# Splits of the weight chunks queued behind the building of the down activations in a fused encoder block

## The chip, the cores and the metric

The kernel runs on one core of one Trainium2 chip, in one launch. The metric is the device time of that launch in microseconds (us), lower is better. Several runs were timed, and one further execution was taken with the hardware profiler.

## The reference

One residual block over 512 tokens of width 1024, all in float32. `rms_norm` divides a row by its root mean square and multiplies by a gain.

```
f = swiglu(rms_norm(h, g_ffn1_pre), w_ffn1_gate, w_ffn1_up, w_ffn1_down)
h = h + 0.5 * rms_norm(f, g_ffn1_post)
u = rms_norm(h, g_mix_pre);  q_a, k_a, v_a, q_b, k_b, v_b = split(u @ w_in)
o_a = stick_breaking_attention(q_a, k_a, v_a);  o_b = chunk_band_attention(q_b, k_b, v_b, rel_bias)
h = h + rms_norm(concat(rms_norm(o_a), rms_norm(o_b)) @ w_out, g_mix_post)
f = swiglu(rms_norm(h, g_ffn2_pre), w_ffn2_gate, w_ffn2_up, w_ffn2_down)
h = h + 0.5 * rms_norm(f, g_ffn2_post)
h = h + rms_norm((p @ w_ple_proj) * sigmoid(h @ w_ple_gate), g_ple_post)

swiglu(x, wg, wu, wd) = (silu(x @ wg) * (x @ wu)) @ wd      # 1024 -> 2816 -> 1024
```

The change touches the two feed-forward stages, called FFN1 and FFN2 here; both go through the same code.

## The kernel before

**Precision.** Each float32 operand is split into a high part, rounded to the fast matmul format fp32r, and a low part, the rest. `split_to` (L311) makes both: ScalarE (ACT) casts the high part (L313), then VectorE (DVE) subtracts it from the source to get the low part (L314). `mm3` (L247) issues three matmuls on TensorE (PE): high weights by high activations (L248), high by low (L249), low by high (L250). The low part of a weight is therefore first needed by the third matmul of a product.

**Weight chunks.** Weights come in chunks of 128 x 1024 (some 128 x 768). `emit_dma` (L168) loads a chunk from SyncE's queue (SP) into a raw tile `wr`, `wx` or `wy`; `emit_split` (L192) splits it into `wh` and `wl`, of which there are four buffers each. Some chunks are sums of weight blocks: once the raw tile has been split, `sum_in` (L222) issues a DMA from GpSimd's queue (POOL, L223) that adds another block into the same raw tile, and the result is split again as a later chunk. `ensure` (L227) issues loads and splits ahead of use; it is called at the end of each product, for the chunk three products ahead (`LOOK`, L25).

**The products.** The 22 blocks of 128 hidden columns of a feed-forward are worked in four groups (L39): four plain blocks, then nine pairs of blocks. A pair's gate and up projection is a 2 x 2 block product in the seven-product form, operands `U0` to `U6`; each product is 24 matmuls of 128 x 256. The products of one pair, in the order 0, 1, 2, 4, 3, 6, 5 (L44), are interleaved with those of the next pair: after product 5 of pair p come product 4 of pair p+1, product 0 of pair p+2, product 3 of pair p+1, product 1 of pair p+2, product 6 of pair p+1. PE runs its instructions in exactly this order. Products 0, 3, 6 and 5 of a pair accumulate in one PSUM bank (`f_a`), product 1 uses `f_b`, products 2 and 4 use `f_c`.

After certain products the banks are read out: L592 and L593 (gate, first half), L596, L599 (`f_x`: ACT copies `f_c`, DVE adds `f_a`), L605, and after product 5 the SiLU of L609 and the multiplication of L646, which completes `f_b`, the hidden activations of the pair (DVE tile `f_b`, not the PSUM bank). A product that accumulates again into a bank has to wait until its reader is done: product 6 waits for L599, product 5 for L605.

**Building the down activations.** The down projection of the middle two groups, three pairs each, also goes by seven products, run from `down_product` (L626). Its activation operands `V` are built by `keep_blocks` (L486), once for each of the six pairs and twice in the kernel: a split of the halves `b4[:, 0::2]` (L499, two tiles of 128 x 256, possible as soon as L646 has written the first half, some products earlier), four differences `f_vw` on DVE (L501 to L503, one after the other), the split of these four into `f_v` (L504, 128 x 1024) and a split of one block into `f_vsl` or `f_vsh` (L505, 128 x 256). The operands of the first two pairs of a group are used many products later; those of the third pair begin to be used two products after product 5 of that pair, since product 0 of the down projection comes after product 4 of the next pair. If the operands of the group before are still in use, the split work of a pair waits for them (`kept`, L563); that is so for the fourth pair, the first of the second group.

**What sets the order.** Only PE's order is written out by hand. On ACT, DVE and POOL a scheduler picks the order from a model of the timeline at build time, and each engine then runs its instructions in that order. `behind` (L321) adds the rule that the instructions inside it stand, on the same engine, after given ones; it adds no wait between engines. `emit_split` uses it so that a chunk's split stands behind `marks["evac"]`, the read-out of the latest product:

```
        for q in range(cuts):
            a, b = q * n // cuts, (q + 1) * n // cuts
            with behind("evac"):
                marks["split"] = split_to(hi[:, a:b], lo[:, a:b], r[:, a:b])
```

The functions that the change touches, and what calls them:

## Time and profile before

| | us |
|---|---|
| median of three runs | 1000.22 |
| lowest and highest of the three | 997.71 and 1000.41 |
| the profiled execution, its own time | 1002.25 |
| its span, first to last instruction | 1000.5 |

The time holds 1.75 us outside the span of the profiled execution. In that span FFN1's pairs and down products run from about 64 to 260 us and those of FFN2 from about 655 to 860 us; attention lies between. The names in a row are the program's tiles with buffer numbers left out: `wl<-wx,wh` is the low part of a chunk, made from its raw tile and its high part. A row of the timeline gives start, duration, engine, line, operation, output and inputs, and in brackets how long the engine stood idle before it and what it waited for. The next instruction of DVE or ACT often starts some 0.1 us before the end of the one before, if it doesn't need its result.

### The profile page before, as it was taken

How to read it: one execution, taken by the hardware profiler on the slowest of the kernel's cores; microseconds unless marked ns; L12 is line 12 of the kernel's file. 1: busy time of each engine (PE TensorE's matmuls, PEld its weight loads, DVE VectorE, ACT ScalarE, POOL GpSimd, SP SyncE). 2: the span in 40 equal slices, each digit the busy share in tenths (PEclk: the TensorE clock that was granted, in tenths of full speed). 3: DMA queues.
4: the chain of work that ended last, by engine and by line, in shares of the span. 5: the costliest groups of instructions: out<-in, count | busy, mean ns of one | idle time of the engine just before them, and what ended most of it. 6: DMA issues, size and time to landing. Idle time of an engine off the chain costs nothing.

```text
span 1000.5 us, 18453 instructions
## 1 busy us (share of the span) xinstructions
PE 980.4 (98%) x7242; PEld 922.5 (92%) x7242; DVE 775.3 (77%) x1357; ACT 585.8 (59%) x979; POOL 134.5 (13%) x221
## 2 busy tenths in 40 slices
PE   9999999999999999999999999999999999999996
PEld 7889999999999999888898899899999999999885
DVE  6777787677667788999999767796776787676857
ACT  6446654564455467777789655565643664555563
POOL 0001112122210004343000000011122122210000
PEclk9999999999999999999999999999999999999999
DMA  7348888988896132313332402269789888975202
GB/s 280 102 106 189 170 188 183 207 181 177 211 191 206 60 82 88 89 61 102 99 89 92 139 10 65 61 142 204 149 186 204 181 169 212 195 180 185 64 1 85
DMA packets 44855, 139.71 MB, mean 140 GB/s; under 512 B 5216, under 2 KB 5600, under 8 KB 44768
## 3 DMA queue, kind: packets, MB, share of 16 engines
q0 software_dynamic: 14976, 50.34, 30.5%
q1 hardware_dynamic: 28368, 85.83, 25.3%
q10 hardware_dynamic: 1424, 2.36, 0.9%
q8 instruction: 57, 0.93, 0.4%
q14 instruction: 30, 0.25, 0.1%
HBM read 134.31 MB, written 2.10 MB: 136 GB/s over the span
## 4 chain that ended last, share of the span: by engine, by line
PE 75%; DMA 8%; DVE 8%; ACT 4%; issue 4%; POOL 0%; SPq 0%; DVEq 0%; POOLq 0%; ACTq 0%
PE f_a L248 7%; PE f_a L250 7%; PE f_a L249 7%; PE f_c L248 3%; PE f_c L250 3%; PE f_c L249 3%; PE pj L248 3%; PE pj L249 3%; PE pj L250 3%; DMA wy<-in_wst_dram 3%; DVE wl L314 2%; PE pt L937 2%; PE f_d L250 2%; PE f_d L249 2%; PE f_d L248 2%
## 5 line engine op out<-in xcount | busy, mean ns | idle before, releaser
L314 DVE TENSOR_TENSOR wl<-wx,wh 128x1024 fp32r<-128x1024 f32 (+1 forms) x104 | 118.3, 1139 | 39.6 <-ACT wh L313 38.7
L313 ACT CAST wh<-wx 128x1024 fp32r<-128x1024 f32 (+1 forms) x104 | 101.8, 985 | 68.1 <-DMA wx<-in_wst_dram 37.4
L314 DVE TENSOR_TENSOR wl<-wr,wh 128x1024 fp32r<-128x1024 f32 (+2 forms) x100 | 109.3, 1099 | 28.8 <-ACT wh L313 28.1
L313 ACT CAST wh<-wr 128x1024 fp32r<-128x1024 f32 (+2 forms) x100 | 94.3, 950 | 46.0 <-DMA wr<-in_wgu_dram 14.0
L223 POOL DMA_DIRECT2D wx<-in_wst_dram x54 | 47.1, 872 | 403.8 <-DVE wl L314 339.5
L313 ACT CAST wh<-wy 128x1024 fp32r<-128x1024 f32 (+1 forms) x52 | 51.4, 988 | 47.5 <-DMA wy<-in_wdst_dram 23.7
L314 DVE TENSOR_TENSOR wl<-wy,wh 128x1024 fp32r<-128x1024 f32 (+1 forms) x52 | 59.2, 1139 | 15.8 <-ACT wh L313 15.2
L248 PE MATMUL pj<-um_hi,wh 128*128 128x512 f32 (+1 forms) x160 | 56.7, 355 | 1.2 <-DVE f_f L658 1.1
L249 PE MATMUL pj<-um_lo,wh 128*128 128x512 f32 (+1 forms) x160 | 55.7, 348 | 0.1
L250 PE MATMUL pj<-um_hi,wl 128*128 128x512 f32 (+1 forms) x160 | 55.8, 348 | 0.0
L248 PE MATMUL f_a<-f_U6h,wh 128*128 128x256 f32 x144 | 40.0, 278 | 2.0 <-DVE f_x L599 1.3
L248 PE MATMUL f_a<-f_U0h,wh 128*128 128x256 f32 x144 | 40.0, 278 | 0.0
L249 PE MATMUL f_a<-f_U0l,wh 128*128 128x256 f32 x144 | 39.8, 277 | 0.0
L250 PE MATMUL f_a<-f_U0h,wl 128*128 128x256 f32 x144 | 39.8, 277 | 0.0
L248 PE MATMUL f_b<-f_U1h,wh 128*128 128x256 f32 x144 | 39.8, 277 | 0.0
L249 PE MATMUL f_b<-f_U1l,wh 128*128 128x256 f32 x144 | 39.8, 277 | 0.0
L250 PE MATMUL f_b<-f_U1h,wl 128*128 128x256 f32 x144 | 39.8, 277 | 0.0
L248 PE MATMUL f_c<-f_U2h,wh 128*128 128x256 f32 x144 | 39.8, 277 | 0.0
L249 PE MATMUL f_c<-f_U2l,wh 128*128 128x256 f32 x144 | 39.8, 277 | 0.0
L250 PE MATMUL f_c<-f_U2h,wl 128*128 128x256 f32 x144 | 39.8, 277 | 0.0
L248 PE MATMUL f_a<-f_U5h,wh 128*128 128x256 f32 x144 | 39.8, 277 | 0.0
L249 PE MATMUL f_a<-f_U5l,wh 128*128 128x256 f32 x144 | 39.8, 277 | 0.0
(461 smaller groups left out, 3851.3 us busy)
## 6 DMA issues: line engine op xcount, KB each, us to landing
wx<-in_wst_dram POOLq DMA_DIRECT2D x54, 512.0 KB, 5.7
wx<-in_wst_dram SPq DMA_DIRECT2D x18, 512.0 KB, 4.9
wy<-in_wst_dram SPq DMA_DIRECT2D x18, 512.0 KB, 5.8
wr<-in_wst_dram SPq DMA_DIRECT2D x18, 512.0 KB, 5.8
wy<-in_wst_dram POOLq DMA_DIRECT2D x18, 512.0 KB, 5.8
wx<-in_wdst_dram POOLq DMA_DIRECT2D x24, 384.0 KB, 5.5
wr<-in_wqk_dram SPq DMA_DIRECT2D x16, 512.0 KB, 3.7
wr<-in_wgu_dram SPq DMA_DIRECT2D x15, 512.0 KB, 4.2
```

Of the source, the lines that this page charges most:

```text
L223: pool.dma_start(out=r, in_=block, accum_op=ALU.add)
L248: pe.matmul(ps, hi, mh, start=start, stop=False, skip_group_check=skip)
L249: pe.matmul(ps, hi, ml, start=False, stop=False, skip_group_check=skip)
L250: pe.matmul(ps, lo, mh, start=False, stop=stop, skip_group_check=skip)
L313: a = act.copy(hi, src)
L314: b = dve.tensor_tensor(lo, src, hi.bitcast(F32), ALU.subtract)
L937: pe.transpose(pt[:, qi * P:(qi + 1) * P], aw[qi][:, (j - qi) * P:(j - qi + 1) * P], ident[:])
```

## The change

```
@@ emit_split
         for q in range(cuts):
             a, b = q * n // cuts, (q + 1) * n // cuts
-            with behind("evac"):
+            with behind("evac", "kept"):
                 marks["split"] = split_to(hi[:, a:b], lo[:, a:b], r[:, a:b])
@@ keep_blocks
-            split_to(e2[:, 0], e2[:, 1], b4[:, 0::2])
+            parts = split_to(e2[:, 0], e2[:, 1], b4[:, 0::2])
             w = half4(unit(f"vw{g}{r}", "b", 3))
             dve.tensor_tensor(w[:, 0:2], b4[:, 0::3], b4[:, 1:2].broadcast_to([P, 2, HT]), ALU.subtract)
             dve.scalar_tensor_tensor(w[:, 2], w[:, 1], -1.0, b4[:, 0], ALU.mult, ALU.subtract)
             dve.scalar_tensor_tensor(w[:, 3], w[:, 2], -1.0, b4[:, 2], ALU.mult, ALU.subtract)
-            split_to(e4[:, 0], e4[:, 1], w)
-            split_to(e1[:, 0], e1[:, 1], b4[:, 3:4])
+            parts += split_to(e4[:, 0], e4[:, 1], w)
+            marks["kept"] = parts + split_to(e1[:, 0], e1[:, 1], b4[:, 3:4])
```

Every split of a weight chunk that is traced after a call of `keep_blocks` now stands, on ACT and on DVE, behind the three casts and the three low parts of that call. No instruction is added or removed and no size changes. PE, POOL and SP keep their orders; ACT and DVE get new ones around ten of the twelve builds, and in the two builds of a fourth pair only the small split of L505 moves up, ahead of one chunk's split.

On ACT, after the product 5 of the first pair of FFN1 (the SiLU of L609), the rows are these; `wh_1070` is the chunk of the product 3 that comes three products later, `wh_1099` and `wh_1128` those of the two products after it:

```order
 L609 ACTIVATE f_g_1050<-f_a_667 128x512
+L313 CAST f_vsl_1056<-f_b_920 128x256
+L599 COPY f_x_1156<-f_c_994 128x512
+L313 CAST f_v_1053<-f_vw_1060 128x1024
 L313 CAST wh_1070<-wx_762 128x1024
 L313 CAST wh_1099<-wr_1068 128x1024
-L313 CAST f_vsl_1056<-f_b_920 128x256
 L313 CAST wh_1128<-wy_956 128x1024
-L599 COPY f_x_1156<-f_c_994 128x512
 L313 CAST wh_1161<-wx_987 128x1024
-L313 CAST f_v_1053<-f_vw_1060 128x1024
```

The casts of the build, and with them the read-out `f_x` of the next pair's bank `f_c`, have moved ahead of the four chunks.

On DVE at the same place, behind L501 of the build, `wl_1071` is the low part of that first chunk:

```order
+L314 TENSOR_TENSOR f_vsl_1056<-f_b_920,f_vsl_1056 128x256
+L502 SCALAR_TENSOR_TENSOR f_vw_1060<-f_vw_1060,f_b_920 128x256
+L503 SCALAR_TENSOR_TENSOR f_vw_1060<-f_vw_1060,f_b_920 128x256
+L314 TENSOR_TENSOR f_v_1053<-f_vw_1060,f_v_1053 128x1024
 L314 TENSOR_TENSOR wl_1071<-wx_762,wh_1070 128x1024
-L502 SCALAR_TENSOR_TENSOR f_vw_1060<-f_vw_1060,f_b_920 128x256
 L314 TENSOR_TENSOR wl_1100<-wr_1068,wh_1099 128x1024
-L314 TENSOR_TENSOR f_vsl_1056<-f_b_920,f_vsl_1056 128x256
-L503 SCALAR_TENSOR_TENSOR f_vw_1060<-f_vw_1060,f_b_920 128x256
 L314 TENSOR_TENSOR wl_1129<-wy_956,wh_1128 128x1024
-L314 TENSOR_TENSOR f_v_1053<-f_vw_1060,f_v_1053 128x1024
 L599 TENSOR_TENSOR f_x_1156<-f_a_864,f_x_1156 128x512
```

The whole build now stands ahead of the three low parts that it was woven into, and the read-out L599 stays behind all of them.

On DVE in the build of the third pair of FFN1, again behind L501, the down projection's accumulation L637 comes in as well; `wl_1539` is the chunk of the product 3 three products later:

```order
+L314 TENSOR_TENSOR f_vsh_1057<-f_b_1393,f_vsh_1057 128x256
+L502 SCALAR_TENSOR_TENSOR f_vw_1528<-f_vw_1528,f_b_1393 128x256
+L503 SCALAR_TENSOR_TENSOR f_vw_1528<-f_vw_1528,f_b_1393 128x256
+L314 TENSOR_TENSOR f_v_1054<-f_vw_1528,f_v_1054 128x1024
+L637 TENSOR_TENSOR f_f<-f_f,f_a_0_1571 128x2x256
 L314 TENSOR_TENSOR wl_1539<-wx_1226,wh_1538 128x1024
-L502 SCALAR_TENSOR_TENSOR f_vw_1528<-f_vw_1528,f_b_1393 128x256
 L314 TENSOR_TENSOR wl_1568<-wr_1536,wh_1567 128x768
-L314 TENSOR_TENSOR f_vsh_1057<-f_b_1393,f_vsh_1057 128x256
-L503 SCALAR_TENSOR_TENSOR f_vw_1528<-f_vw_1528,f_b_1393 128x256
-L637 TENSOR_TENSOR f_f<-f_f,f_a_0_1571 128x2x256
 L314 TENSOR_TENSOR wl_1592<-wy_1429,wh_1591 128x1024
```

Here L637, which reads the result of the down projection's first product, has moved ahead of `wl_1539` too.

## The prediction

> **What bounds the kernel now.** I read the page's busy times first, then a table by stage, then what PE waited for in the two feed-forwards.

> ```profile
> span 1000.5 us, 18453 instructions
> PE 980.4 (98%) x7242; PEld 922.5 (92%) x7242; DVE 775.3 (77%) x1357; ACT 585.8 (59%) x979; POOL 134.5 (13%) x221
> ```

> PE is the bound; the next, DVE, has a fifth of the span free. By stage (busy PE, PEld, DVE, ACT, POOL, then granted clock, DMA share, GB/s):

> ```profile
> 64.00:260.00 196.00, 195.24 (x1660) 192.89 (x1659) 151.34 (x186) 107.71 (x142) 36.86 (x43) 1.00 0.85 185
> 640.00:860.00 220.00, 216.62 (x1792) 212.06 (x1791) 166.60 (x205) 117.61 (x155) 39.45 (x46) 1.00 0.82 178
> ```

> PE is idle for 0.8 us of FFN1's stretch and 3.4 us of FFN2's. Almost nothing can be won there: whatever frees other engines is worth at most 4.1 us. But whatever delays PE counts in full. The waits of PE, first in FFN1's stretch, then in FFN2's (total, times, longest):

> ```profile
> PE f_a L248 <- DVE f_x L599: 0.4, 1, 0.4
> PE f_c L248 <- ACT f_y L596: 0.2, 1, 0.2
> ...
> PE f_a L248 <- DVE f_f L637: 1.4, 1, 1.4
> PE f_a L248 <- DVE f_x L599: 0.9, 1, 0.9
> PE f_a L248 <- ACT f_g L592: 0.7, 1, 0.7
> PE f_c L248 <- ACT f_y L596: 0.4, 1, 0.4
> ```

> PE never waits there for a weight chunk. So the question is how early the chunks are ready, and by how much the change delays them. The first build of FFN1 on DVE:

> ```profile
> 102.66 0.69 DVE L646 SCALAR_TENSOR_TENSOR f_b<-f_y,f_g 128x512 f32<-128x512 f32 x1 [0.56 <-ACT f_g L609]
> 103.39 0.69 DVE L501 TENSOR_TENSOR f_vw<-f_b 128x512 f32<-128x512 f32 x1
> 104.00 1.22 DVE L314 TENSOR_TENSOR wl<-wx,wh 128x1024 fp32r<-128x1024 f32 x1
> 105.13 0.42 DVE L502 SCALAR_TENSOR_TENSOR f_vw<-f_vw,f_b 128x256 f32<-128x256 f32 x1
> 105.47 1.22 DVE L314 TENSOR_TENSOR wl<-wr,wh 128x1024 fp32r<-128x1024 f32 x1
> ...
> 106.94 0.42 DVE L503 SCALAR_TENSOR_TENSOR f_vw<-f_vw,f_b 128x256 f32<-128x256 f32 x1
> 107.28 1.22 DVE L314 TENSOR_TENSOR wl<-wy,wh 128x1024 fp32r<-128x1024 f32 x1
> 110.23 1.23 DVE L314 TENSOR_TENSOR f_v<-f_vw,f_v 128x1024 fp32r<-128x1024 f32 x1 [1.73 <-ACT f_v L313]
> 111.37 0.68 DVE L599 TENSOR_TENSOR f_x<-f_a,f_x 128x512 f32<-128x512 f32 x1
> ```

> and on ACT:

> ```profile
> 102.03 0.60 ACT L609 ACTIVATE f_g<-f_a 128x512 f32<-128x512 f32 x1 [1.19 <-PE f_a L250]
> 102.53 1.04 ACT L313 CAST wh<-wx 128x1024 fp32r<-128x1024 f32 x1
> ...
> 104.41 0.41 ACT L313 CAST f_vsl<-f_b 128x256 fp32r<-128x256 f32 x1
> ...
> 105.79 0.58 ACT L599 COPY f_x<-f_c 128x512 f32<-128x512 f32 x1
> 108.19 1.05 ACT L313 CAST wh<-wx 128x1024 fp32r<-128x1024 f32 x1 [1.82 <-DMA wx<-in_wst_dram]
> 109.15 1.05 ACT L313 CAST f_v<-f_vw 128x1024 fp32r<-128x1024 f32 x1
> ```

> and on PE, the last matmul of product 4 and the second and third of product 3:

> ```profile
> 104.48 0.28 PE L250 MATMUL f_c<-f_U4h,wl 128*128 128x256 f32 x1
> ...
> 107.42 0.28 PE L249 MATMUL f_a<-f_U3l,wh 128*128 128x256 f32 x1
> 107.54 0.28 PE L250 MATMUL f_a<-f_U3h,wl 128*128 128x256 f32 x1
> ```

> The chunk of product 3 has its low part at 104.00 + 1.22 = 105.22, and the matmul that needs it starts at 107.54: a lead of 2.32 us. That is all the room there is, since a chunk is split only after the read-out of the product three places before its own.

> **Part by part.** No instruction is added, so all cost is delay.

> *First kind of build* (first and second pair of a group). I replay the new order with these durations, from the unmoved L646 on. L501 ends at 104.08. The cast of `f_vsl` on ACT waits for L646 (103.35), so it is done at 103.8 and its low part follows L501 at once, 104.00 to 104.42. L502 starts 0.34 later (as after 105.13) at 104.34 and ends at 104.76. L503 needs its result; with the 0.04 between L646 and L501 it runs 104.80 to 105.22. ACT meanwhile meets the copy `f_x`, which needs product 4's last matmul (104.48 + 0.28 = 104.76): 104.79, and the next cast may start 0.48 later, at 105.27. So the cast of `f_v` runs 105.27 to 106.32, and its low part on DVE 106.35 to 107.58. The chunk's cast starts 0.96 after `f_v`'s, 106.23 to 107.28, still in time for the first matmul of product 3. But its low part starts only 1.14 after `f_v`'s (110.23 to 111.37), at 107.49, and ends at 108.71: 3.49 later than before, against a lead of 2.32. PE lacks 1.17, plus some 0.05 for the signal and 0.1 for the weight load, which otherwise lies under the matmul before it: **1.3 us**. The next two low parts end at 109.85 and 111.0; their products start, with PE 1.3 later, well after that (24 matmuls 0.12 apart, so 2.8 each). L599 then waits for product 3 itself and not for the build. So one wait per build, not three.

> This occurs three times in each feed-forward: first and second pair of the first group and second pair of the second. For the fourth pair only the small split moves up (0.4 us on each engine), which I cost at nothing to 0.4 and take as nothing, since the orders show one chunk behind it and PE shows no wait for a chunk there. Six times 1.3 is 7.8 us.

> *Second kind* (third pair of a group). Product 3 comes sooner here, because the product before it is the down projection's, with 18 matmuls in place of 24:

> ```profile
> 141.55 0.69 DVE L501 TENSOR_TENSOR f_vw<-f_b 128x512 f32<-128x512 f32 x1
> 142.16 1.22 DVE L314 TENSOR_TENSOR wl<-wx,wh 128x1024 fp32r<-128x1024 f32 x1
> ...
> 145.17 0.68 DVE L637 TENSOR_TENSOR f_f<-f_f,f_a 128x512 f32<-128x512 f32 x1
> ...
> 142.64 0.28 PE L250 MATMUL f_c<-f_U4h,wl 128*128 128x256 f32 x1
> ...
> 144.70 0.28 PE L250 MATMUL f_a<-f_vsh,wl 128*128 128x256 f32 x1
> 145.05 0.28 PE L250 MATMUL f_a<-f_U3h,wl 128*128 128x256 f32 x1
> ```

> The lead was 145.05 - 143.38 = 1.67. By the same steps `f_v`'s low part starts 2.96 after L501 (106.35 against 103.39), at 144.51, and the next instruction at 145.65. That is L637, whose product has by then ended (144.70 + 0.28 = 144.98); its 0.68, 0.08 of it overlapped, puts the chunk's low part at 146.25 to 147.47. PE lacks 2.42, with the same 0.15 **2.55 us**. Twice in each feed-forward: 10.2 us.

> *What goes.* The waits of product 6 for L599 in the first builds of the same kinds (0.9 in FFN2, 0.4 in FFN1) and, as I take it, that of 0.7 for L592 come from L599 standing behind an `f_v` that stood behind a cast waiting for a DMA (the 1.73 and 1.82 above). In the new order `f_v` waits for no chunk. That takes off 2.0 us. The waits for L637 (1.4) and L596 (0.2 and 0.4) lie away from the builds; I leave them.

> *What is late next: the sum DMAs.* POOL issues the add into a raw tile after the low part, so 3.5 us later too, and product 5 needs the sum. From the trace, an add, its landing times (min, median, max), and product 5 of either kind of build:

> ```profile
> 105.57 0.88 POOL L223 DMA_DIRECT2D wx<-in_wst_dram  x1 [2.23 <-DVE f_vw L502]
> ...
> DMA to landing us min/median/max: 4.7/5.7/10.9
> ...
> 118.19 0.28 PE L248 MATMUL f_a<-f_U5h,wh 128*128 128x256 f32 x1
> ...
> 154.39 0.28 PE L248 MATMUL f_a<-f_U5h,wh 128*128 128x256 f32 x1
> ```

> After landing come cast (1.05), low part (next start 1.14 later) and the read-out L605 behind it on DVE (0.69), on which product 5 waits: some 2.9. In the first kind the add starts at 109.06 and product 5 at 118.19 + 1.3 = 119.49, so a landing within 7.5 us is in time. In the second kind the low part ends at 147.47, the add starts at 147.8 and product 5 at 154.39 + 2.55 = 156.94: 6.2 us are allowed. The median, 5.7, fits both; I take nothing.

> Sum: 7.8 + 10.2 - 2.0 = **16.0 us**. The profiled execution took 1002.25 us, so 1018.25 on its scale; it lies 2.03 above the median of 1000.22, and on the median's scale the forecast is **1016.2 us**.

> **Rivals.**

> *The leads hold, and only the gain is left.* If DVE and ACT get through the build 1.2 us sooner than I chain it, the delay stays inside 2.32 and PE pays nothing; the 2.0 us of waits go. The point that decides is whether low part `wl` of product 3 ends by 107.5. For it: DVE does lose time behind `f_v` now. Against it: every link of my chain is a result that the next one needs. It gives 998.2, and 996.4 if the two further waits in FFN2 (1.4 and 0.4) shrink as well. Second kind, with 1.67, would still have to hold. Chance 0.06.

> *The adds land late.* FFN2's own row shows a slow one:

> ```profile
> 693.79 0.88 POOL L223 DMA_DIRECT2D wx<-in_wst_dram  x1 [2.25 <-DVE f_vw L502]
> ...
> 702.80 1.06 ACT L313 CAST wh<-wx 128x1024 fp32r<-128x1024 f32 x1 [1.05 <-DMA wx<-in_wst_dram]
> ```

> That is 9.0 us, 1.5 over the first kind's allowance and 2.8 over the second's. If FFN2's five builds all met it, 3 x 1.5 + 2 x 2.8 = 10.1 more: 1026. Against it: the DMA share is 0.82 to 0.85, and PE's own waits give the queues time. Chance 0.13.

> *PE's clock drops after the waits.* If each wait of the second kind cost one product at half speed (24 matmuls, 0.12 apart, 2.8 us more), four would add 11: 1027. The rows speak against it: the clock is 1.00 over FFN2's stretch, with a wait of 1.4 in it; none there is as long as 2.55. [...] Chance 0.03.

> **How the numbers follow.** The forecast has the remaining chance, 0.78. Its own range: 1.0 and 2.2 for the two waits, and all of the 4.0 us of present waits gone, give 6 + 8.8 - 4.0 = 10.8, 1011; 1.5 and 2.9, only 1.3 gone and 2 us of late adds, give 9 + 11.6 + 0.7 = 21.3, 1021.5. The range reaches to the late adds above and a little below: 1009 to 1026. A difference under 0.3% (3 us) can't be told from no change. Slower by more: the forecast, late adds and the clock less a little, 0.92; within: 0.05, nearly all from leads that hold; faster by more: 0.03.

> **What would show it.** PE should wait, in ten places, at the third matmul of product 3 for `wl` L314: six times about 1.3 us and four times about 2.5; the waits of product 6 for L599 should be gone, and DVE's for `f_v` should fall to the bare cast. The low part `wl` should start about 4.1 us after L501 in the first kind and 4.7 in the second, where it was 0.6. I am wrong in the size if PE waits at other products too (product 5 for L605, which means the adds), and wrong in kind if there is no such wait, or if it lies at the casts `wh`.

## The result, and the profile after

The changed kernel takes 1027.76 us (median of 6 runs, 1024.61 to 1032.1) against 1001.5 us (6 runs, 997.71 to 1004.51): ratio 1.0268, 95% interval [1.0232, 1.0304]. It is slower, as forecast, but by 26 us where 16.0 were forecast, and outside the range. Its profiled execution took 1031.54 us. The page's first lines:

```profile
span 1029.8 us, 18463 instructions
...
PE 992.2 (96%) x7242; PEld 932.3 (91%) x7242; DVE 777.4 (75%) x1357; ACT 585.1 (57%) x979; POOL 134.6 (13%) x221
```

The span is 29.3 us longer than before. DVE, ACT and POOL are as busy as they were, within 2.1 us. PE, with the same matmuls, is busy 11.8 us longer: some of them took longer than before (0.41 and 0.42 us in the rows at 151.12 and 151.32 below, where the mean was 0.28 before), so waits are not all of it. What PE waited for on the banks `f_a` and `f_c` (total, times, longest):

```profile
PE f_a L250 <- DVE wl L314: 11.8, 10, 1.5
PE f_a L248 <- DVE f_y L605: 4.4, 2, 2.3
PE f_a L248 <- ACT wh L313: 2.2, 5, 0.5
PE f_a L248 <- DVE f_f L637: 1.7, 1, 1.7
PE f_c L248 <- DVE f_f L637: 0.5, 1, 0.5
```

The first row is the forecast's: ten waits of the third matmul for `wl`. The waits for L599 and L592 are gone. The rows for L605 and for the cast `wh` are new; of the waits for L637, the one of 1.4 in FFN2 is gone and one of 1.7 has come in FFN1. The first build of FFN1 on DVE:

```profile
102.67 0.69 DVE L501 TENSOR_TENSOR f_vw<-f_b 128x512 f32<-128x512 f32 x1
...
105.64 1.23 DVE L314 TENSOR_TENSOR f_v<-f_vw,f_v 128x1024 fp32r<-128x1024 f32 x1 [1.15 <-ACT f_v L313]
106.78 1.22 DVE L314 TENSOR_TENSOR wl<-wx,wh 128x1024 fp32r<-128x1024 f32 x1
```

`wl` starts 4.11 us after L501; 4.1 was worked out. On PE, the third matmul of product 3 in this build, and the same product in the build of FFN1's third pair:

```profile
108.06 0.38 PE L250 MATMUL f_a<-f_U3h,wl 128*128 128x256 f32 x1 [0.94 <-DVE wl L314]
...
148.04 0.38 PE L248 MATMUL f_a<-f_U3h,wh 128*128 128x256 f32 x1 [0.51 <-ACT wh L313]
148.26 0.28 PE L249 MATMUL f_a<-f_U3l,wh 128*128 128x256 f32 x1
150.09 0.39 PE L250 MATMUL f_a<-f_U3h,wl 128*128 128x256 f32 x1 [1.54 <-DVE wl L314]
...
150.89 0.28 PE L250 MATMUL f_a<-f_U3h,wl 128*128 128x256 f32 x1
151.00 0.31 PE L248 MATMUL f_a<-f_U3h,wh 128*128 128x256 f32 x1
151.12 0.41 PE L249 MATMUL f_a<-f_U3l,wh 128*128 128x256 f32 x1
151.32 0.42 PE L250 MATMUL f_a<-f_U3h,wl 128*128 128x256 f32 x1
```

The third pair's wait falls into two: 0.51 for the cast and 1.54 for the low part. Then, 1.0 us after the second wait, the spacing of the matmuls goes from 0.12 to 0.21 with nothing to wait for. The table by stretch shows the granted clock, its third number from the end, going down at the same place:

```profile
148.00:150.00 2.00, 0.50 (x2) 0.30 (x2) 2.00 (x4) 2.00 (x3) 0.00 (x0) 1.00 0.00 0
150.00:152.00 2.00, 1.91 (x13) 1.91 (x14) 2.00 (x3) 0.40 (x1) 0.86 (x1) 0.78 0.13 8
152.00:154.00 2.00, 2.00 (x11) 2.00 (x11) 0.04 (x1) 0.00 (x0) 0.00 (x0) 0.50 0.95 137
154.00:156.00 2.00, 2.00 (x17) 2.00 (x17) 1.66 (x3) 0.00 (x0) 0.00 (x0) 0.87 1.05 266
```

The granted clock is 0.50 for 3.4 us. That occurs four times in the two feed-forwards: from 151.1 and 243.3 in the product 3 behind FFN1's two third pairs, and from 765.5 and 861.1 at the product 5 behind FFN2's. And the first third pair's add in FFN2: its issue and its cast in the kernel before, then, in the changed kernel, from its issue to the product that needs it:

```profile
734.03 0.88 POOL L223 DMA_DIRECT2D wx<-in_wst_dram  x1 [2.70 <-DVE f_vw L502]
739.91 1.06 ACT L313 CAST wh<-wx 128x1024 fp32r<-128x1024 f32 x1 [2.27 <-DMA wx<-in_wst_dram]
...
754.14 0.88 POOL L223 DMA_DIRECT2D wx<-in_wst_dram  x1 [6.96 <-DVE wl L314]
...
762.74 1.05 ACT L313 CAST wh<-wx 128x1024 fp32r<-128x1024 f32 x1 [8.59 <-DMA wx<-in_wst_dram]
...
764.97 0.68 DVE L605 TENSOR_TENSOR f_y<-f_a,f_y 128x512 f32<-128x512 f32 x1
...
765.80 0.55 PE L248 MATMUL f_a<-f_U5h,wh 128*128 128x256 f32 x1 [2.34 <-DVE f_y L605]
```

The cast runs 8.6 us after the issue where it was 5.9, the low part and L605 follow, and PE waits 2.34. In the other three builds of the second kind it is 8.3 (FFN2), 7.3 and 7.8 (FFN1).

PE runs the same matmuls in the same order in both kernels, so each can be paired with itself, and the 29.3 us fall to the places where the distance grows:

| place | forecast | measured |
|---|---|---|
| product 3, first kind of build, six times (1.33 each) | 7.8 | 8.0 |
| product 3, second kind, four times (2.58 each) | 10.2 | 10.3 |
| present waits that go (0.63, 1.18, 0.89) | -2.0 | -2.7 |
| half clock, four stretches of 3.4 us (1.4 to 1.6 each) | 0 | 6.0 |
| product 5 behind the late add, FFN2's third pairs (2.62, 2.33) | 0 | 4.9 |
| down projection, waits for L637 and the step behind it, new less gone | 0 | 0.2 |
| some 23 products with their matmuls 0.118 apart in place of 0.113 | 0 | 2.6 |
| all the rest | 0 | 0.0 |

A wait counts here with the slower matmuls next to it: of the 1.33, 1.10 to 1.12 fall to the matmul that waits and 0.1 each to the one ahead of it and the one behind. The row of 2.6 belongs to neither kernel alone. In four stretches of 18 to 20 us of the two feed-forwards PE starts its matmuls a little further apart, at a granted clock of 1.00 (104 from 110 to 122 us, where it started 108 before). Paired in the same way, the other profiles have 0.7 to 3.0 us of this, and a second profile of the kernel before 2.0. Its cause stays open.

### The profile page after: what moved, and what is told of

It reads as the page before. It is cut to its first block, busy times and chain, and to the rows that moved or that the text cites. A ratio compares the mean times of both kernels' runs of the same rounds, so it can differ in the third digit from the quotient of the medians.

```text
span 1029.8 us, 18463 instructions
## 1 busy us (share of the span) xinstructions
PE 992.2 (96%) x7242; PEld 932.3 (91%) x7242; DVE 777.4 (75%) x1357; ACT 585.1 (57%) x979; POOL 134.6 (13%) x221
## 3 DMA queue, kind: packets, MB, share of 16 engines
q0 software_dynamic: 14976, 50.34, 29.3%
## 4 chain that ended last, share of the span: by engine, by line
PE 77%; DVE 8%; DMA 7%; issue 4%; ACT 4%; POOL 0%; DVEq 0%; ACTq 0%; SPq 0%; POOLq 0%
PE f_a L250 7%; PE f_a L248 7%; PE f_a L249 7%; PE f_c L248 3%; PE f_c L250 3%; PE f_c L249 3%; PE pj L248 3%; PE pj L249 3%; PE pj L250 3%; DVE wl L314 3%; DMA wy<-in_wst_dram 2%; PE pt L937 2%; PE f_d L249 2%; PE f_d L250 2%; PE f_d L248 2%
## 5 line engine op out<-in xcount | busy, mean ns | idle before, releaser
L314 DVE TENSOR_TENSOR wl<-wx,wh 128x1024 fp32r<-128x1024 f32 (+1 forms) x104 | 118.4, 1140 | 55.2 <-ACT wh L313 53.7
L313 ACT CAST wh<-wx 128x1024 fp32r<-128x1024 f32 (+1 forms) x104 | 102.0, 984 | 76.2 <-DMA wx<-in_wst_dram 49.7
L314 DVE TENSOR_TENSOR wl<-wr,wh 128x1024 fp32r<-128x1024 f32 (+2 forms) x100 | 109.3, 1099 | 27.8 <-ACT wh L313 27.0
L313 ACT CAST wh<-wr 128x1024 fp32r<-128x1024 f32 (+2 forms) x100 | 94.3, 950 | 46.8 <-DMA wr<-in_wgu_dram 13.3
L223 POOL DMA_DIRECT2D wx<-in_wst_dram x54 | 47.1, 872 | 416.2 <-DVE wl L314 410.8
L313 ACT CAST wh<-wy 128x1024 fp32r<-128x1024 f32 (+1 forms) x52 | 51.2, 985 | 36.5 <-DMA wy<-in_wst_dram 17.3
L314 DVE TENSOR_TENSOR wl<-wy,wh 128x1024 fp32r<-128x1024 f32 (+1 forms) x52 | 59.2, 1138 | 13.8 <-ACT wh L313 13.8
L248 PE MATMUL pj<-um_hi,wh 128*128 128x512 f32 (+1 forms) x160 | 56.8, 355 | 1.3 <-DVE f_f L658 1.1
L249 PE MATMUL pj<-um_lo,wh 128*128 128x512 f32 (+1 forms) x160 | 55.6, 348 | 0.1
L250 PE MATMUL pj<-um_hi,wl 128*128 128x512 f32 (+1 forms) x160 | 55.7, 348 | 0.0
L250 PE MATMUL f_a<-f_U3h,wl 128*128 128x256 f32 x144 | 42.5, 295 | 11.8 <-DVE wl L314 11.8
L248 PE MATMUL f_a<-f_U5h,wh 128*128 128x256 f32 x144 | 41.8, 290 | 4.4 <-DVE f_y L605 4.4
L248 PE MATMUL f_a<-f_U3h,wh 128*128 128x256 f32 x144 | 42.3, 294 | 2.0 <-ACT wh L313 2.0
L249 PE MATMUL f_a<-f_U5l,wh 128*128 128x256 f32 x144 | 41.4, 287 | 0.0
L249 PE MATMUL f_a<-f_U3l,wh 128*128 128x256 f32 x144 | 41.2, 286 | 0.0
L250 PE MATMUL f_a<-f_U5h,wl 128*128 128x256 f32 x144 | 41.2, 286 | 0.0
L250 PEld LDWEIGHTS f_a<-f_U3h,wl 128*128 128x128 f32 x144 | 28.5, 198 | 13.9 <-DVE wl L314 13.9
L248 PE MATMUL f_a<-f_U0h,wh 128*128 128x256 f32 x144 | 40.0, 278 | 0.2 <-ACT wh L313 0.2
L248 PE MATMUL f_b<-f_U1h,wh 128*128 128x256 f32 x144 | 40.0, 278 | 0.0
L249 PE MATMUL f_b<-f_U1l,wh 128*128 128x256 f32 x144 | 40.0, 278 | 0.0
L250 PE MATMUL f_b<-f_U1h,wl 128*128 128x256 f32 x144 | 40.0, 278 | 0.0
L248 PE MATMUL f_c<-f_U2h,wh 128*128 128x256 f32 x144 | 40.0, 278 | 0.0
```

The lines of the kernel that those rows point to most:

```text
L223: pool.dma_start(out=r, in_=block, accum_op=ALU.add)
L248: pe.matmul(ps, hi, mh, start=start, stop=False, skip_group_check=skip)
L249: pe.matmul(ps, hi, ml, start=False, stop=False, skip_group_check=skip)
L250: pe.matmul(ps, lo, mh, start=False, stop=stop, skip_group_check=skip)
L313: a = act.copy(hi, src)
L314: b = dve.tensor_tensor(lo, src, hi.bitcast(F32), ALU.subtract)
```

## The experiments

The theory: the forecast's sum for product 3 holds, and what it lacks are two consequences of the third pair's long stall, the half clock and the late add. Rivals: the stalls at product 3 themselves were mis-sized, or all builds share the excess alike. Some expectations go by slightly different sizes of the same terms: 7.2, 10.3, -2.2, 6.3 and 5.0.

**Only the first kind of build.** The splits stand behind the build for the first two pairs of a group alone:

```
-            marks["kept"] = parts + split_to(e1[:, 0], e1[:, 1], b4[:, 3:4])
+            parts += split_to(e1[:, 0], e1[:, 1], b4[:, 3:4]); marks["kept"] = parts if r < 2 else ()
```

> The rule is kept for the first and second pair of a group (first kind of build) and dropped for the third pair. Theory (the cost is the delayed chunk of product 3, and all that came beyond the forecast hangs on the third pair's long wait): six waits of 1.2 us, less the two waits of 1.0 and 0.7 us that go, so +5.5 us on the kernel before; the clock stays at full speed throughout and product 5 does not wait. Rival (the surplus of some 10 us is spread over all ten builds, six of them here): +14 us or more, with slower matmuls or half clock after the short waits too.

Measured: 1007.04 us against 1000.8, ratio 1.0059 [1.0037, 1.008], some 6 us (5.9 by the ratio). PE's waits on the two banks:

```profile
PE f_a L250 <- DVE wl L314: 5.7, 6, 0.9
PE f_a L248 <- DVE f_f L637: 2.3, 2, 1.2
```

Six waits of 0.94 and none for L605; the clock is never at half in the two feed-forwards (its mean over the span is 0.998, as in the kernel before). This kind of build does what the sum said (7.8 less the 2.0 of waits that go) and has no part in the excess from half clock and late adds.

**Only the second kind.** The same line, for the third pair:

```
+            parts += split_to(e1[:, 0], e1[:, 1], b4[:, 3:4]); marks["kept"] = parts if r == 2 else ()
```

> The rule is kept for the third pair of a group alone. Theory: four waits of 2.5 us, the clock at half for some 3.4 us after about four long waits (1.6 us each), two waits of product 5 in FFN2 (2.3 to 2.6 each), and 1 to 2 us in the down projection: +20 to +23 us. Rival (spread): four tenths of the whole, +10 to +12 us, with no half clock.

Measured: 1019.89 us against 1000.8, ratio 1.0177 [1.0149, 1.0206].

```profile
PE f_a L250 <- DVE wl L314: 6.2, 4, 1.5
PE f_a L248 <- DVE f_y L605: 2.9, 4, 1.0
PE f_a L248 <- DVE f_f L637: 2.9, 2, 1.8
PE f_a L248 <- ACT wh L313: 2.0, 4, 0.5
```

The four stalls alone are the forecast's 10.2; the rest is the new rows for L605 and L637 and two stretches at half clock, both in FFN2 (mean clock 0.994). It fell just short of the 20 expected (19.1 by medians), with two stretches in place of four. FFN1 has none here, and there product 5 waits for L605 too, 0.77 and 0.80. The excess belongs to the third pairs. The two halves together give 25 us by medians and 24 by ratios, the whole change 26 and 27.

**The long waits filled.** In the changed kernel, idle matmuls ahead of product 3 behind each third pair, and in FFN2 ahead of product 5 there, whose results nothing reads; the orders of the other engines stay as they are:

```
+        def fill_wait(op, p):
+            if p in (3, 6) and (op == 3 or op == 5 and name == "f2"):
+                ps = psum("T", f"{name}_fill{op}{p}", HT)
+                for _ in range(16):
+                    pe.matmul(ps[:], U[0][0][0][:, :P], U[0][0][0], start=True, stop=True, skip_group_check=True)
```

`fill_wait(op, p)` is called at the head of a product. The lines behind it move by six (L605 is L611).

> The changed kernel, with 16 idle matmuls of 128 x 256 (about 1.9 us, into an unused bank, results not read) put on PE ahead of product 3 after each third pair, and ahead of product 5 there in FFN2, where PE waits anyway. Theory (the half clock comes from PE being idle): no stretch at half clock, about four times 1.6 us less than the changed kernel, so +20 us on the kernel before; the chunks are as late as ever. Rival (the half clock has another cause, or the matmuls merely run slower for want of data): half clock stays, +26 us or more.

Measured: 1024.91 us, ratio 1.0223 [1.0182, 1.0263]; the span is 1023.4, and there is no stretch at half clock in the two feed-forwards (mean clock 0.998).

```profile
PE f_a L250 <- DVE wl L314: 7.2, 10, 0.9
PE f_a L248 <- DVE f_y L611: 3.9, 3, 2.0
```

`wl` and the add come no sooner, PE only stays busy while they are late. The half clock is gone, but not all of its 6.0 us: the kernel gains 2.9 by medians and 4.5 by the ratios, so the time lies between the two expectations. Product 5 behind FFN1's third pairs now waits 1.06 and 1.97, where it waited for nothing in the changed kernel. There the adds were late too (7.3 and 7.8 for the 6.2 allowed), and the slow stretch ahead of product 5 had hidden it.

**The late add left out.** In `emit_split`, four adds aren't issued:

```
-                sum_in(r[:, :n], src[add[0], add[1]])
+                sum_in(r[:, :n], src[add[0], add[1]]) if not (op == 3 and item in ((3,), (6,))) else None
```

> The changed kernel without the DMA add into the raw tile of product 3 of the pair that follows each third pair (four adds in all; products 5 of those pairs then use an incomplete sum). Theory (product 5 waits since the add is issued and lands late): the two waits of product 5 in FFN2 are gone, 5 us less, and with them up to two stretches at half clock (3 us): +18 to +21 us on the kernel before. Rival (product 5 waits for DVE or ACT being behind with their own work): the waits stay and the time is +26 us.

Measured: 1020.65 us, ratio 1.0181 [1.0147, 1.0216], as the theory expected.

```profile
PE f_a L250 <- DVE wl L314: 11.8, 10, 1.5
PE f_a L248 <- ACT wh L313: 2.2, 5, 0.5
PE f_a L248 <- DVE f_f L637: 0.4, 1, 0.4
```

Product 3 waits as before, the row for L605 is gone and that for L637 nearly so. Two stretches at half clock are left, one in each feed-forward (mean clock 0.995).

**Both taken away.** The add left out, and 16 idle matmuls ahead of product 3 alone:

```
-            if p in (3, 6) and (op == 3 or op == 5 and name == "f2"):
+            if p in (3, 6) and op == 3:
```

> The changed kernel with both terms that the forecast missed taken away: the four late adds left out, and 16 idle matmuls (128x256) ahead of each product 3 that follows a third pair, so that PE runs through most of its wait there. Sums incomplete, as without the late adds. Theory (half clock 6.3 us, late adds 5.0 and 2 us behind them in the down projection): what is left is the forecast's own sum, 7.2 + 10.3 - 2.2, some 15 us over the kernel before, ratio 1.013 to 1.017, no stretch at half clock, no wait for L605. Rival (the two terms are not the whole, and the fillers and the left-out adds each only took noise): 18 us or more, no better than either alone, ratio 1.018 or over.

Measured: 1016.84 us against 997.81, ratio 1.0186 [1.0156, 1.0215]; 10.7 below the kernel of the next experiment, which ran on the same chip.

```profile
PE f_a L250 <- DVE wl L314: 7.2, 10, 0.9
PE f_a L248 <- DVE f_y L611: 0.4, 1, 0.4
```

No half clock is left in the two feed-forwards (mean clock 0.998), and next to no wait for L605 (L611 here). The ratio lies at the rival's edge and its interval holds both, so it decides nothing. Paired with the profiled execution of before, the span is 14.8 us longer: 8.0 at the first kind and 10.3 at the second, less 2.7 of waits that go and 0.8 elsewhere. The kernel before ran shorter in this comparison (997.81) than in its own profile (1002.25), and where those 4 us lie was not profiled.

**Half the filling.** 8 idle matmuls in place of 16, at the six places of the first filling:

```
-                for _ in range(16):
+                for _ in range(8):
```

> The changed kernel with 8 idle matmuls in place of 16 at the same six places, so that about 0.9 us of each long wait is covered and 1.2 to 1.7 us of PE's idle time is left there. Theory (a half-clock stretch follows only when some 2 us or more of idle time lie close together): no half-clock stretch, or one at most; mean granted clock 0.997 or more, time near that with 16 matmuls, ratio 1.019 to 1.025. Rival (a single wait of about 1.5 us is enough): two or more stretches at half clock, clock 0.995 or less, ratio 1.024 or more.

Measured: 1027.51 us against 997.81, ratio 1.0296 [1.0261, 1.0331]. One stretch at half clock (mean clock 0.996), as the theory said, but the time is the rival's: it went to three late adds.

```profile
PE f_a L250 <- DVE wl L314: 11.1, 10, 1.4
PE f_a L248 <- DVE f_y L611: 6.7, 3, 2.4
```

More telling are two product 5 of one execution, one of FFN1 and one of FFN2:

```profile
254.63 0.36 PE L248 MATMUL f_a<-f_U5h,wh 128*128 128x256 f32 x1 [2.43 <-DVE f_y L611]
254.82 0.28 PE L249 MATMUL f_a<-f_U5l,wh 128*128 128x256 f32 x1
...
764.27 0.36 PE L248 MATMUL f_a<-f_U5h,wh 128*128 128x256 f32 x1 [2.38 <-DVE f_y L611]
...
764.93 0.40 PE L250 MATMUL f_a<-f_U5h,wl 128*128 128x256 f32 x1
765.13 0.41 PE L248 MATMUL f_a<-f_U5h,wh 128*128 128x256 f32 x1
```

After a wait of 2.43 the spacing stays at 0.12, after one of 2.38 it goes to 0.21. So the length of the wait alone did not decide here. In each execution all changes of the granted clock lie on one grid: in the changed kernel the four stretches start 92.16, 522.24 and 95.57 us apart, 27, 153 and 28 times 3.4133. The wait of 2.38 lay whole in one window of that grid; of that of 2.43 no window held more than 1.70.

**Both kernels profiled again**, unchanged.

> The kernel before, unchanged, in a second profiled execution, to see whether the waits that the sum took off (0.9, 0.7, 0.4) and those behind the down projection's first products (1.4, 0.7) belong to the kernel or to one execution. Theory (they come and go with the landing times of the transfers, and make the difference between its shorter and longer executions, some 4 us): an execution of 997 to 999 us shows at most 1 us of waits in the two feed-forwards, one of 1001 to 1003 shows 3 to 5 us. Rival (they are fixed by the order): the same waits at the same products, within 0.3 us, whatever the time.

Measured: 1005.46 us for the kernel before, above the executions that the expectation speaks of: 2.5 us of waits for L599 and L637, 1.9 of them for L599 (L599 and L592 had 2.0 in the first profile), but 0.6 for L637 in place of 1.4. Neither expectation fits. New is a stretch at half clock that the first profile hadn't, with two waits in FFN1's last block; together they cost 4.4 us, paired with the first profile, of which 1.2 come back elsewhere:

```profile
302.90 0.50 PE L248 MATMUL f_d<-f_sh,f_e0h 128*128 128x512 f32 x1 [1.33 <-ACT f_sh L313]
304.35 0.79 PE L249 MATMUL f_d<-f_sl,f_e0h 128*128 128x512 f32 x1 [0.95 <-DVE f_sl L314]
304.94 0.63 PE L250 MATMUL f_d<-f_sh,f_e0l 128*128 128x512 f32 x1
```

> The changed kernel, unchanged, in a second profiled execution. Theory: the ten waits of product 3 are set by the order and come again within 0.2 us each (six of 0.9, four of 0.5 with 1.5); the waits for L605 come again in the third pair's builds of FFN2, within 0.5 us, since the add is always issued late there; the stretches at half clock, two to four of 3.4 us, come again, each behind a pair of waits close together, though not all at the same places. Rival (the four stretches are set by the order as well): four stretches at the same four products.

Measured: 1027.46 us for the changed kernel.

```profile
PE f_a L250 <- DVE wl L314: 11.9, 10, 1.5
PE f_a L248 <- DVE f_y L605: 3.0, 2, 2.3
PE f_a L248 <- ACT wh L313: 2.2, 5, 0.5
...
751.33 0.87 POOL L223 DMA_DIRECT2D wx<-in_wst_dram  x1 [6.96 <-DVE wl L314]
...
759.89 1.05 ACT L313 CAST wh<-wx 128x1024 fp32r<-128x1024 f32 x1 [8.55 <-DMA wx<-in_wst_dram]
...
762.95 0.36 PE L248 MATMUL f_a<-f_U5h,wh 128*128 128x256 f32 x1 [0.69 <-DVE f_y L605]
```

The ten waits come again to a tenth. The two for L605 come at the same products, but the first is shorter, 0.69 in place of 2.34. Four stretches at half clock again, three at the same products and one in a product 3 where it was at a product 5. The last two belong together: the add was as late as before (8.6 us from issue to cast in both), but this time the half clock came ahead of product 5, and its 1.6 us hid that much of the lateness. The theory holds but for the first wait for L605.

**The limit tested.** The executions so far suggested that a stretch follows a window with 1.90 us or more of idle PE time. Two and four idle matmuls at the six places were to put it just over and just under (`range(2)` and `range(4)` in the same line).

> Two idle matmuls (0.23 us) in place of 16 at the six places. In the executions so far every change of the granted clock lies on one grid of 3.413 us within an execution, and a half-clock stretch of 3.41 us followed each window of that grid in which PE stood idle 1.90 us or more (gaps between the starts of matmuls of over 0.45 us, less 0.2), and no window with 1.80 or less. Theory (the idle time in a window of the grid decides): no exception here; the waits at product 3 of a third pair leave some 1.9 to 2.0 us of idle time, just over the limit, so a stretch follows where the whole of it lies in one window, and none where it is cut to less than 1.8. Rival (it is the length of a wait, or the place): a stretch behind a window of 1.7 us or less, or none behind one of 2.0 or more.

> Four idle matmuls (0.46 us) in place of 16 at the six places. Theory (the idle time in a window of the 3.413 us grid decides, with a limit between 1.80 and 1.90): the waits at product 3 of a third pair leave 1.7 to 1.8 us, just under the limit, and no half-clock stretch follows any of them; those of product 5 for L605, where they are over 2.2 us and lie whole in one window, may still bring one. No exception to the limit in some 290 windows. Rival (the length of a wait, or the place): a stretch behind a product 3 of a third pair with 1.7 us or less in its window.

Measured, one run each: 1026.32 and 1024.65 us, against one run of 1004.13. The grid and the length of 3.41 us held, the limit did not: three stretches each, behind windows with 1.97, 1.97 and 1.71 us in the first and 1.62 three times in the second. That is the rival's sign, though a wait of the same length at the same place, 1.54 in a window with 1.62, brought none in the changed kernel. Over the 14 profiled executions, 290 to 300 windows each up to the last matmul: all 16 windows with 1.90 or more are followed by a stretch, none with 1.56 or less is, and of twelve between 1.62 and 1.80 four are. If only the idle time is counted that the rows give ahead of a matmul, the two groups overlap less: all 16 with 1.80 or more, none with 1.56 or less, and four of six between 1.57 and 1.73. So in these executions the limit lies between 1.56 and 1.90; half a window, 1.71, is the author's estimate from these counts. What decides near it stays open.

**Fewer chunks moved.** If the stall of product 3 is the cost, sparing its chunk should save nearly all. In `keep_blocks` the count of chunks split so far is stored, and `emit_split` obeys the rule only from a later chunk on:

```
-            with behind("evac", "kept"):
+            with behind("evac", *(["kept"] if i >= kept_at[0] + 1 else [])):
```

> The rule does not hold for the first chunk split after a build (that of product 3), only from the second on. Theory (the cost is the first chunk's lead): that chunk is in time; the second chunk had a lead of 3.6 us and is pushed back by some 3.4 us, so PE waits little or not at all, 0 to 0.3 us per build of the first kind; after a third pair the second chunk had 3.2 and may lack up to 1 us. The waits for L599 of the kernel before (2 us in all) go. Between -2 and +4 us on the kernel before, no half clock. Rival (any rule that weaves the build apart from the chunks costs, for the queue's length stays the same): +10 us or more.

Measured: 1001.35 us against 1001.19, ratio 1.0005 [0.9991, 1.0019]: no difference, as the theory allowed, and no wait for `wl` at product 3. With `+ 3` in place of `+ 1`, so from the fourth chunk:

> The rule holds from the fourth chunk after a build on, so only the cast that waits for a DMA moves behind the build. Theory: no chunk of the first three is delayed, the waits of product 6 behind L599 (0.9, 0.7 and 0.4 us) go, and the time falls by 2 us (0.2%), which may not be told from no change; in the profile those three waits are missing. Rival (those waits have another cause than the queue behind the late cast): they stay, and so does the time.

Measured: 998.1 us, ratio 0.9968 [0.9954, 0.9981], 3.2 us faster than the kernel before by the ratio, where 2 were expected, and the only kernel here that is faster. All that PE waits for on `f_a` and `f_c` is:

```profile
PE f_a L248 <- DVE f_f L637: 1.4, 2, 0.7
```

The waits for L599 and L592 are gone and nothing has come in their place.

## Why the prediction was right and wrong

- *The replay of the first kind: right.* The low part of the chunk was put at 107.49; in the trace it starts 4.11 after L501 where that makes 4.10. PE lost 1.33 for the 1.3 forecast. The 0.05 for the signal and the 0.1 for the weight load were put down without a row; in the trace the third matmul starts 0.06 after `wl` ends (108.00 to 108.06) and takes 0.38 in place of 0.28. The experiment with this kind alone gave +5.9 by ratio for 7.8 - 2.0.
- *The replay of the second kind: right in the sum, not in its parts.* 2.55 was forecast, 2.58 measured. But the cast `wh` is late too, by 0.51; that it comes in time was worked out for the first kind alone, and a wait at the casts was named as a sign of being wrong in kind. The total is unchanged, since the low part behind it sets the end; two waits instead of one matter only for the clock.
- *What goes: right*, 2.0 in waits and 2.7 with the slower matmuls behind them, for 2.0. The second profile of before has 1.9 again, so it belongs to the kernel, and moving the one late cast took it away.
- *"The median, 5.7, fits both; I take nothing": wrong for the second kind.* The allowance of 6.2 was sound, the landing was not: 5.7 is the median of all 104 adds of the kernel before, and the new order was taken to leave it as it is. In the seven profiles in which the third pair's chunk is late, the four adds of the second kind land 6.9 to 9.5 us after their issue, all 28 of them; in the five others that have these adds 5.4 to 6.6, with one of 8.3. In the changed kernel it is 7.2, 7.7, 8.5 and 8.2. Less the 6.2, and less the 1.5 that a stretch at half clock ahead of product 5 gives in FFN1, that makes waits of 0, 0, 2.3 and 2.0. PE waited 2.34 and 2.06 in FFN2, 4.9 with what follows a wait, and not in FFN1. The rival had the late adds, at 0.13, with 2.8 for each, but took them from a slow add of the first kind; no first-kind build met it. Why they land later is not shown. In the changed order the next two loads are issued 0.5 and 1.7 us after the add, in the kernel before 0.9 and 3.3. That the second load holds the add up would fit, but no run tests it.
- *The rival of the clock, at 0.03: rated too low.* This is the step that failed most, 6.0 us. The evidence quoted against it, a clock of 1.00 over FFN2 with a wait of 1.4 in it, showed only that 1.4 was too little there; that 2.55 would be too little as well was not shown, and the chance was the author's estimate. In the changed kernel the waits of 0.51 and 1.54 together were enough: with 1.97 us of idle time in one 3.41 us window, a stretch at half clock followed. Its price was also off, since a stretch cost 1.4 to 1.6 and not 2.8: each of the four lasted 3.4 us, two in a product 3 and two at a product 5.
- *The two are not independent.* Both follow from the third pair's stall, and a stretch at half clock ahead of product 5 hid 1.5 of a late add in FFN1. Either left out leaves the forecast too low by about 5 or more. Each alone stays inside the range (1009 to 1026), together they pass it.

## What to carry to other kernels

When work is queued ahead of something the bound engine needs, replay the queue against the lead of the first consumer; done with rows of the trace, that came out within 0.1 us per instruction here. Then go on past the first wait. Here the stall delayed an add with 0.5 us to spare, and the add itself took 7.2 to 8.5 us to land in place of the 5.7 put in, so a duration measured in the old order was no safe term. And gaps that added up to 1.90 us or more in one 3.41 us window were each time followed by a stretch at half clock, at 1.4 to 1.6 us in the changed kernel. An order rule is best applied only to what can afford it: the same rule from the fourth chunk on was faster than both kernels (ratio 0.9968 to the kernel before).
